# Moving SBUF tiles to one start modulo 512 bytes

## The chip, the core and the metric

The kernel runs on one core of one Trainium2 chip. The metric is device time in microseconds (us), from runs of the whole kernel. TensorE (PE) multiplies matrices and loads their stationary operands ("weight loads", PEld), VectorE is DVE, ScalarE is ACT, GpSimd is POOL, and SP issues most DMA transfers. SBUF is the on-chip memory: 128 partitions, in each of which every tile has the same start address and the same number of bytes. A "position" below is a tile's start address modulo 512 bytes.

## The reference

One layer of a decoder trunk on 1024 tokens of width 1024, all in float32. Two branches read the normed input, gates merge them, and a second gated input is added:

```python
h = rms_norm(x, g_pre[i])
proj = h @ w_in[i]
s5_x, s5_g, lru_x, lru_g, gate_s, gate_l = jnp.split(proj, IN_SPLITS, axis=-1)
y_s = s5_ssm(s5_x, ...)                       # 32 groups of 16 channels, 64 complex states each
glu_a, glu_b = jnp.split(jax.nn.gelu(y_s) @ w_glu[i], 2, axis=-1)
y_s = glu_a * jax.nn.sigmoid(glu_b) * jax.nn.silu(s5_g)
z_s = y_s @ w_bs[i]
c = causal_depthwise_conv(lru_x, conv_w[i], conv_b[i])
y_l = rg_lru(c, ...)                          # 10 heads of 128 channels, two 128x128 gates each
z_l = (y_l * jax.nn.silu(lru_g)) @ w_bl[i]
merged = jax.nn.sigmoid(gate_s) * z_s + jax.nn.sigmoid(gate_l) * z_l
x = x + rms_norm(merged @ w_out[i], g_post[i])
x = x + (p[i] @ w_ple[i]) * jax.nn.sigmoid(x @ w_ple_gate[i])
```

## The kernel before

**Matmuls.** Channels lie on the partitions and tokens along the free axis, in two halves of 512. Every large operand is split into a high and a low part (float32r), and each product is made of three matmuls by the helper `three` (lines 314 to 318): high weight by high operand (L316), then high by low and low by high (both L318). Such a matmul has a stationary block `wq` of 128x128 and a moving operand of 128x512. TensorE runs them one after another, in the order in which the code is written; while one streams, the weights of the next are loaded.

**Stages**, in the trace's order: `ps_ple` (the second input's product) to 25 us; the norm; `ps_u` and `ps_L` (input projection, S5 part and light gates) from 38 to 325 us, with the S5 scan between them; `ps_rx`/`ps_rg` (the LRU branch, head by head) to 565 us, with two gate products `pg` in each head that read the tile `chl`; the back projections `bX`, `bZ`, `bW`, `bV`, with the GLU `ps_eb`/`ps_ea` between them, to 711 us; `ps_F` to 755 us; the output projection `oX` to `oW`, with seven-product schemes that read sums of quarters (`bT`, `mT`, `bB`, `mB`); and the last gate `ps_pg`, which reads `x1hl`, one half of the tokens after the other.

**S5.** For each of 8 groups of heads, `s5_main` gives TensorE three short sets of plain float32 matmuls between those of `ps_L`: `pkt` (L925, reads `ca` and `bb`), `pin` (L936, reads `U` and the page `wn`) and `py` (L980 and L981, reads `U`, `toep`, `q` and `ca`).

**Where tiles lie.** Pools take SBUF from two ends. From the low end come the reserved DMA area (16384 bytes), four small constants, the pool `const` (`ones`, `ident`, `halfpi`, `cp_t` and two more), the raw weights `wraw`, the split weights `wq` (a ring of 6 tiles of 4096 bytes) and 14 pages of 8192 bytes. After `tc.swap_default_side()` pools take space from the high end downward, from address 229344: first the S5 pools `sk`, `ev` and `wk`, later, once these are closed, `l1` (the LRU's tiles, `chl` among them), then the pages 14 to 18. A tile takes its own bytes, rounded up to 32. So a tile that is not a multiple of 512 bytes shifts the position of all tiles behind it. These are the starts modulo 512 of what TensorE reads, from the allocation of the built program:

| operand | read by | before | after the change |
|---|---|---|---|
| `wq` (all weight blocks of `three`) | every 128x512 matmul | 160 | 480 |
| pages 0 to 13: `hB`, `ys`, `mB`, `yl`, geo0 and geo1, most of `bT`, `bB`, `x1hl` | `ps_L`, `ps_rx`, `ps_rg`, `ps_F` and others | 160 | 480 |
| `chl` | `pg` | 480 | 480 |
| pages 14 to 18: geo2 and geo3, T2 of `bT`, B22 of `bB`, T2 and T4 of `mT` | half of `ps_eb` and `ps_ea`; one product in each scheme | 480 | 480 |
| low part of `x1hl` for the second gate half (pages 14, 15) | `ps_pg` from 881 us | 480 | 480 |
| `U`, `q` | `pin`, `py` | 256 | 480 |
| `wn` (pages 2, 3) | `pin` | 160 | 480 |
| `toep` | `py` | 480 | 480 |
| `ca` (slices 576 bytes apart, some 64 further on) | `pkt`, `py` | tiles at 256 and 0 | tiles at 480 |
| `bb` (slices 64 bytes apart) | `pkt` | 288 | 480 |
| `ones`, `ident` | warm-up, norm sums | 128 | 448 |

The low and high parts of `wq`, and the 512-element quarters of a page, are whole multiples of 512 bytes apart and share their tile's position.

Of the kernel before, what the change touches and what calls it, by code (L numbers as in the profile page):

```python
# [9 lines left out]
F32 = mybir.dt.float32  # L10
# [7 lines left out]
P = 128  # L18
NT = 1024
HT = 512  # L20
# [115 lines left out]
class Weights:  # L136
# [99 lines left out]
    def next(self):  # L236
        self.make(self.pos)
        self.lows(self.pos)
        t = self.done[self.pos]
        n = QUADS[self.pos][3]  # L240
        self.pos += 1
        return [(t[:, 0, b, :], t[:, 1, b, :]) for b in range(n)]
# [10 lines left out]
def tile_hybrid_trunk(  # L253
# [34 lines left out]
    def cst(shape, name, value=None, dt=F32):  # L288
        t = const.tile(shape, dt, name=name)
        if value is not None:  # L290
            V.memset(t, value)
        return t

    ones = cst([P, P], "ones", 1.0)
    ident = cst([P, P], "ident")
    make_identity(nc, ident)
# [26 lines left out]
    def bank(name):  # L323
        return pp.tile([P, HT], F32, tag="pp", name=name)
# [131 lines left out]
    sk = s5x.enter_context(tc.tile_pool(name="sk", bufs=1))  # L456
# [22 lines left out]
    ET = mybir.EngineType  # L479
    ctx.enter_context(tc.manual_schedule(engines={ET.PE, ET.DVE, ET.Activation, ET.Pool}))  # L480

    sgn = sk.tile([P, 1], F32, name="sgn")
    bb = sk.tile([P, 512], F32, name="bb")
    d_skip = sk.tile([16, 32], F32, name="d_skip")
    r8 = sk.tile([P, 16], F32, name="r8")
    sinp = sk.tile([P, 160], F32, name="sinp")
# [340 lines left out]
    wk = s5x.enter_context(tc.tile_pool(name="wk", bufs=1))  # L827
# [46 lines left out]
    def s5_load(hb):  # L874
        if hb > 7:
            return
        t = page(2 + hb % 2, f"wn{hb}", F32).rearrange("p (s r n) -> p s r n", s=2, r=2)
        for r in range(2):
            nc.sync.dma_start(t[:, 0, r],
                              pt_d[r, :, HT * hb:HT * hb + HT].unsqueeze(0).to_broadcast([16, 8, HT]))  # L880
        nc.sync.dma_start(
            t[:, 1].rearrange("p r n -> p (r n)"),
            sbt[:, NT * hb:NT * hb + NT].unsqueeze(1).to_broadcast([16, 8, NT]))
        U = wk.tile([P, 4, P], F32, tag="U", name=f"U{hb}", bufs=2)
        nc.sync.dma_start(U, u_d[hb // 2][4 * (hb % 2):4 * (hb % 2) + 4].rearrange("g c j k -> (c j) g k"))
        wload[hb] = t, U

    def powers(t, hb, sl):
        return t[:, sl, 4 * hb:4 * hb + 4].rearrange("p d g -> p g d").unsqueeze(3)

    def s5_out_weights(hb):
        if hb == 0:
            G.tensor_tensor(cc[:, 0], cc[:, 0], sgn.to_broadcast([P, 512]), ALU.mult)
        ca = wk.tile([P, 4, 9, 16], F32, tag="ca", name=f"ca{hb}", bufs=2)
        s5["ca", hb] = ca
        t9 = wk.tile([P, 576], F32, tag="kt", name=f"t9_{hb}").rearrange("p (g d c) -> p g d c", g=4, d=9)
        pr, pi = (powers(t, hb, slice(0, 9)).to_broadcast([P, 4, 9, 16]) for t in (pw_r, pw_i))
        c1, c2 = (t[:, 4 * hb:4 * hb + 4, :].unsqueeze(2).to_broadcast([P, 4, 9, 16]) for t in (c_1, c_2))
        G.tensor_tensor(ca, pr, c1, ALU.mult)
        G.tensor_tensor(t9, pi, c2, ALU.mult)  # L900
        G.tensor_tensor(ca, ca, t9, ALU.subtract)

    def s5_main(hb, table, before):
        b, i0, g0 = hb // 2, 2 * hb, 4 * (hb % 2)
        ta = wk.tile([P, 2, 2, P], F32, tag="ta", name=f"ta{hb}")
        tb = wk.tile([P, 2, 2, P], F32, tag="tb", name=f"tb{hb}")
        tt = s5["tt", hb]
        ca = s5["ca", hb]
        wn, U = wload.pop(hb)
        V.tensor_tensor(wn[:, 0], wn[:, 0], wn[:, 1], ALU.mult)  # L910
        win = wn[:, 0, 0].rearrange("p (g n) -> p g n", g=4)
        V.tensor_tensor(wn[:, 0, 0], wn[:, 0, 0], wn[:, 0, 1], ALU.subtract)
        dd = wk.tile([16, 4, 16], F32, tag="dd", name=f"dd{hb}")
        G.tensor_tensor(
            dd, ident[:16, :16].unsqueeze(1).to_broadcast([16, 4, 16]),
            d_skip[:, 4 * hb:4 * hb + 4].unsqueeze(2).to_broadcast([16, 4, 16]), ALU.mult)
        yield
        before()
        s5_load(hb + 1)
        yield  # L920

        kt = wk.tile([P, 576], F32, tag="kt", name=f"kt{hb}")[:16, :HT].rearrange("p (g m) -> p g m", g=4)
        ps = px.tile([P, HT], F32, tag="px", name=f"pkt{hb}")
        for g in range(4):
            T.matmul(ps[32 * g:32 * g + 16, :P], bb_1[:, 4 * hb + g, :],  # L925
                     ca[:, g, 0:8, :].rearrange("p d c -> p (d c)"), start=True, stop=True, tile_position=(0, 32 * g))
        for g in range(4):
            S.activation(kt[:, g, :], ps[32 * g:32 * g + 16, :P], AF.Copy)
        V.tensor_tensor(kt[:, :, 0:16], kt[:, :, 0:16], dd, ALU.add)
        for j in range(8):  # L930
            nc.sync.dma_start(toep[j::8, :, 16 * j:P], kt[:, :, 0:P - 16 * j])
        yield

        pin = px.tile([P, 2, 2, P], F32, tag="px", name=f"pin{hb}")
        for g in range(4):
            T.matmul(pin[:, g // 2, g % 2, :], win[:, g, :], U[:, g, :], start=True, stop=True)  # L936
        next(table, None)
        yield

        pq = wk.tile([P, 4, P], F32, tag="pq", name=f"pq{hb}").rearrange("p (r i) n -> p r i n", r=2)  # L940
        for g2 in range(2):
            for r in range(2):
                S.activation(pq[64 * g2:64 * g2 + 64, r], pin[64 * r:64 * r + 64, :, g2, :], AF.Copy)
        q = wk.tile([P, 2, 2, P], F32, tag="q", name=f"q{hb}")
        cosb = tt[:, 0].unsqueeze(1).to_broadcast([P, 2, 2, P])
        sinb = tt[:, 1].unsqueeze(1).to_broadcast([P, 2, 2, P])
        V.tensor_tensor(ta, pq, cosb, ALU.mult)
        V.tensor_tensor(tb, pq, sinb, ALU.mult)
        V.tensor_tensor(q[:, 0], ta[:, 0], tb[:, 1], ALU.add)
        V.tensor_tensor(q[:, 1], ta[:, 1], tb[:, 0], ALU.subtract)  # L950
        if hb < 7:
            s5_out_weights(hb + 1)
        yield

        for r in range(2):
            for i in range(2):
                V.tensor_tensor_scan(q[:, r, i], r8[:, i0 + i:i0 + i + 1].to_broadcast([P, P]), q[:, r, i], 0.0,
                                     ALU.mult, ALU.add)
        next(table, None)
        e = P - 1  # L960
        V.tensor_tensor(ta, q, cosb, ALU.mult)
        V.tensor_tensor(tb, q, sinb, ALU.mult)
        yield

        V.memset(q[:, :, :, 0:1], 0.0)
        for g2 in range(2):
            s = slice(64 * g2, 64 * g2 + 64)
            V.tensor_tensor(q[:64, :, g2, 1:], ta[s, 0, :, :e], tb[s, 1, :, :e], ALU.subtract)
            V.tensor_tensor(q[64:, :, g2, 1:], ta[s, 1, :, :e], tb[s, 0, :, :e], ALU.add)
        next(table, None)  # L970
        yield

        def finish():
            for _ in table:
                pass
            ysb = wk.tile([P, 4, P], F32, tag="ysb", name=f"ysb{hb}")
            ps = px.tile([P, HT], F32, tag="px", name=f"py{hb}")
            for g in range(4):
                o_ = ps[:, g * P:(g + 1) * P]
                T.matmul(o_, toep[:, g, :], U[:, g, :], start=True, stop=False)  # L980
                T.matmul(o_, ca[:, g, 1:9, :].rearrange("p d c -> p (d c)"), q[:, g // 2, g % 2, :],  # L981
                         start=False, stop=True)
            S.activation(ysb.rearrange("p g k -> p (g k)"), ps, AF.Gelu_apprx_tanh)
            for g in range(4):
                nc.sync.dma_start(y_d[b][:, g0 + g], ysb[:, g])

        return finish
# [319 lines left out]
    for p_ in range(4):  # L1307
        m, u = 2 * p_, bu[:, p_, :]
# [163 lines left out]
    def mixt(row, h):  # L1472
        if mix[h][row // 4] is None:
            mix[h][row // 4] = quarter(page(PG[((0, 2), (18, 11))[h][row // 4]], f"mix{h}{row // 4}", F32))
        return mix[h][row // 4][:, row % 4, :]
# [141 lines left out]
    for name, row in (("T4", 1), ("T4", 3), ("T4", 5), ("T4", 7), ("B21", 4), ("B21", 6)):  # L1617
        c, ps = mixt(row, 0), bank(f"oV{row}")
# [76 lines left out]
```

## Time and profile before

| what | value |
|---|---|
| median of 3 runs | 932.56 us (932.4 to 933.21) |
| profiled execution, first to last instruction (span) | 930.6 us |
| the median less that span (around it: start and end of the execution) | 1.96 us |
| granted TensorE clock, mean | 0.999 of full speed |
| TensorE busy | 923.1 us, 4228 matmuls |
| DVE, ACT, POOL busy | 625.0, 469.6, 150.3 us |
| DMA moved | 134.21 MB, mean 144 GB/s |

The profile lists one execution. For the profiled execution nothing but its span is listed; its full time is taken as the span and the 1.96 us around it. A matmul's own duration there (389 ns and more) is longer than its share of TensorE's time, since each begins while the one before is still draining. What a matmul costs in a row of them is the distance from its start to the start of the next, and that is read from the start times in the timeline.

### The profile page before, as it was taken

The page shows a single profiled execution, that of the slowest core. Times are in us where ns is not written, and L with a number is a line of the kernel's source. Part 1 is how long each engine was busy: PE and PEld are TensorE (multiplying, and loading weights), DVE is VectorE, ACT ScalarE, POOL GpSimd, SP SyncE. Part 2 cuts the span into 40 slices and gives each one's busy share as a digit, 9 for nine tenths or more (in the row PEclk, how much of TensorE's full clock was granted, in tenths as well). Part 3 has the DMA queues.
Part 4 walks back from the last instruction along what each step waited for, and adds up shares of the span by engine and source line. Part 5 has one row for each costly group of instructions (what it writes and reads, how often), then busy time and mean ns, then how long its engine had stood idle before and what let it go on. Part 6 is the DMA issues. An engine that isn't in the chain of part 4 may idle for free.

```text
span 930.6 us, 11716 instructions
## 1 busy us (share of the span) xinstructions
PE 923.1 (99%) x4228; PEld 759.7 (82%) x4228; DVE 625.0 (67%) x977; ACT 469.6 (50%) x714; POOL 150.3 (16%) x159
## 2 busy tenths in 40 slices
PE   9999999999999999999999999999999999999997
PEld 7888888888888888888888888888888887887876
DVE  6985566666664446776666667687862798886863
ACT  6643233444443257666666668444434355558531
POOL 1318012212220000000000000022322126422100
PEclk9999999999999999999999999999999999999999
DMA  9745456554623211111111117811479965499951
GB/s 356 277 126 158 126 141 168 173 166 138 178 90 107 74 29 52 51 51 45 52 51 51 52 44 208 296 41 57 141 261 238 271 164 203 122 244 231 301 181 52
DMA packets 70442, 134.21 MB, mean 144 GB/s; under 512 B 18416, under 2 KB 32880, under 8 KB 70384
## 3 DMA queue, kind: packets, MB, share of 16 engines
q1 hardware_dynamic: 64768, 122.72, 41.5%
q0 software_dynamic: 5472, 10.49, 6.5%
q8 instruction: 33, 0.54, 0.2%
q10 hardware_dynamic: 144, 0.26, 0.1%
q14 instruction: 25, 0.20, 0.1%
HBM read 95.30 MB, written 27.53 MB: 132 GB/s over the span
## 4 chain that ended last, share of the span: by engine, by line
PE 96%; DVE 2%; issue 0%; DMA 0%; ACT 0%
PE ps_L L318 16%; PE ps_L L316 8%; PE ps_rg L318 8%; PE ps_rx L318 8%; PE ps_pg L318 6%; PE ps_rx L316 4%; PE ps_rg L316 4%; PE ps_F L318 3%; PE ps_u L318 3%; PE bZ L318 3%; PE ps_pg L316 3%; PE pg L318 2%; PE bW L318 2%; PE bX L318 2%; PE ps_ple L318 2%; PE ps_ea L318 2%
## 5 line engine op out<-in xcount | busy, mean ns | idle before, releaser
L318 PE MATMUL ps_L<-hB,wq 128*128 128x512 f32 x640 | 197.4, 390 | 0.0
L318 PEld LDWEIGHTS ps_L<-hB,wq 128*128 128x128 f32 x640 | 120.2, 188 | 24.5
L316 PE MATMUL ps_L<-hB,wq 128*128 128x512 f32 x320 | 127.0, 397 | 0.0
L222 ACT ACTIVATE wq<-wraw 128x512 fp32r<-128x512 f32 (+1 forms) x188 | 112.5, 614 | 24.3 <-issue 9.4
L234 DVE TENSOR_TENSOR wq<-wraw,wq 128x512 fp32r<-128x512 f32 (+1 forms) x152 | 104.0, 700 | 3.2 <-ACT wq L222 3.2
L318 PE MATMUL ps_rg<-hB,wq 128*128 128x512 f32 x320 | 98.7, 390 | 0.0
L318 PE MATMUL ps_rx<-hB,wq 128*128 128x512 f32 x320 | 98.7, 390 | 0.0
L318 PE MATMUL ps_pg<-x1hl,wq 128*128 128x512 f32 x240 | 75.2, 394 | 0.5 <-DVE x1hl L1371 0.5
L316 PEld LDWEIGHTS ps_L<-hB,wq 128*128 128x128 f32 x320 | 60.1, 188 | 13.4 <-issue 1.7
L318 PEld LDWEIGHTS ps_rg<-hB,wq 128*128 128x128 f32 x320 | 60.1, 188 | 12.9
L318 PEld LDWEIGHTS ps_rx<-hB,wq 128*128 128x128 f32 x320 | 60.1, 188 | 12.9
L1075 DVE SCALAR_TENSOR_TENSOR c<-ps_rx,cp_t,c 128x1023 f32<-128x1023 f32 (+2 forms) x30 | 38.5, 1282 | 47.6 <-ACT c L1073 46.9
L194 POOL TENSOR_TENSOR wS<-wraw 128x512 f32<-128x512 f32 x8 | 11.9, 1486 | 356.8 <-DMA wraw<-w_blocks 349.4
L316 PE MATMUL ps_rx<-hB,wq 128*128 128x512 f32 x160 | 62.5, 391 | 0.0
L316 PE MATMUL ps_rg<-hB,wq 128*128 128x512 f32 x160 | 62.5, 391 | 0.0
L318 PEld LDWEIGHTS ps_pg<-x1hl,wq 128*128 128x128 f32 x240 | 44.7, 188 | 11.8 <-DVE x1hl L1371 1.8
L1012 ACT ACTIVATE sg<-ps_L 128x1024 f32<-128x1024 f32 x20 | 20.5, 1026 | 59.6 <-issue 52.5
L226 POOL DMA_DIRECT2D wq<-wraw x36 | 31.8, 883 | 100.7 <-ACT wq L225 68.7
L316 PE MATMUL ps_pg<-x1hl,wq 128*128 128x512 f32 x120 | 47.1, 393 | 0.0
L318 PE MATMUL ps_u<-hB,wq 128*128 128x512 f32 x128 | 39.7, 392 | 0.4 <-DVE hB L733 0.4
L318 PE MATMUL ps_F<-ys,wq 128*128 128x512 f32 x128 | 39.4, 389 | 0.0
L1083 ACT ACT_TABLE_LOAD x9 | 11.5, 1283 | 51.2 <-DVE yr L1112 51.2
(360 smaller groups left out, 1930.4 us busy)
## 6 DMA issues: line engine op xcount, KB each, us to landing
wraw<-w_blocks SPq DMA_DIRECT2D x95, 512.0 KB
wq<-wraw POOLq DMA_DIRECT2D x36, 256.0 KB, 5.5
xt<-x_t SPq DMA_DIRECT2D x8, 512.0 KB
ple_d<-ple_sb SPq DMA_DIRECT2D x8, 512.0 KB
wn<-sbt SPq DMA_DIRECT2D x8, 512.0 KB
sgl_d<-sg SPq DMA_DIRECT2D x8, 512.0 KB
wn<-pt_d SPq DMA_DIRECT2D x16, 256.0 KB
sgs_d<-sg SPq DMA_DIRECT2D x8, 512.0 KB
```

What stands on the lines that cost most here:

```text
L194: G.tensor_tensor(s[name], s[a], s[b], op)
L222: nc.scalar.activation(hi, src, AF.Copy)
L226: nc.gpsimd.dma_start(lo.bitcast(F32), src, accum_op=ALU.add)
L234: self.nc.vector.tensor_tensor(lo, src, hi.bitcast(F32), ALU.subtract)
L316: T.matmul(ps, wh, xh, start=start, stop=False, skip_group_check=more)
L318: T.matmul(ps, a, b, start=False, stop=stop and a is (wh if xl_last else wl), skip_group_check=more)
L1012: S.activation(t, ps, AF.Sigmoid)
L1075: V.scalar_tensor_tensor(c[:, d:], ps[:, :NT - d], w_[3 - d], c[:, d:], ALU.mult, ALU.add)
L1083: S.activation(sq, ps, AF.Sigmoid)
```

## The change

A tile `phase` of 80 floats (320 bytes), which nothing uses, is taken from the pool `const` ahead of `ones`, so all that lies behind it on the low side is 320 bytes higher. In the S5 pools the tiles `sgn`, `bb`, `ca`, `kt`/`t9` and `dd` are taken larger and used in part, so that they take whole multiples of 512 bytes (`sgn` and `bb` bring the small tiles of `sk` to such a multiple together).

```diff
+    cst([P, 80], "phase")
     ones = cst([P, P], "ones", 1.0)
...
-    sgn = sk.tile([P, 1], F32, name="sgn")
-    bb = sk.tile([P, 512], F32, name="bb")
+    sgn = sk.tile([P, P], F32, name="sgn")[:, :1]
+    bb = sk.tile([P, 592], F32, name="bb")[:, :512]
...
-        ca = wk.tile([P, 4, 9, 16], F32, tag="ca", name=f"ca{hb}", bufs=2)
+        ca = wk.tile([P, 640], F32, tag="ca", name=f"ca{hb}", bufs=2)[:, :576].rearrange("p (g d c) -> p g d c", g=4, d=9)
...
-        t9 = wk.tile([P, 576], F32, tag="kt", name=f"t9_{hb}").rearrange("p (g d c) -> p g d c", g=4, d=9)
+        t9 = wk.tile([P, 640], F32, tag="kt", name=f"t9_{hb}")[:, :576].rearrange("p (g d c) -> p g d c", g=4, d=9)
...
-        dd = wk.tile([16, 4, 16], F32, tag="dd", name=f"dd{hb}")
+        dd = wk.tile([P, P], F32, tag="dd", name=f"dd{hb}")[:16, :64].rearrange("p (g c) -> p g c", g=4)
...
-        kt = wk.tile([P, 576], F32, tag="kt", name=f"kt{hb}")[:16, :HT].rearrange("p (g m) -> p g m", g=4)
+        kt = wk.tile([P, 640], F32, tag="kt", name=f"kt{hb}")[:16, :HT].rearrange("p (g m) -> p g m", g=4)
```

No instruction is added, removed or moved: on all five queues the same instructions stand in the same order with the same shapes. Only addresses differ.

## The prediction

> **What bounds the kernel.** I read the page first: busy time of the engines, granted clock, and the chain that ended last.
>
> ```profile
> PE 923.1 (99%) x4228; PEld 759.7 (82%) x4228; DVE 625.0 (67%) x977; ACT 469.6 (50%) x714; POOL 150.3 (16%) x159
> PEclk9999999999999999999999999999999999999999
> PE 96%; DVE 2%; issue 0%; DMA 0%; ACT 0%
> ```
>
> TensorE is busy for 99% of the span, at the full clock throughout, and 96% of the chain is TensorE. Next, the view of who waited for whom, for TensorE alone:
>
> ```profile
> PE warm L497 <- DVE halfpi L291: 1.1, 1, 1.1
> PE ps_ple L316 <- ACT wq L222: 0.6, 1, 0.6
> PE ps_pg L318 <- DVE x1hl L1371: 0.5, 1, 0.5
> PE ps_u L318 <- DVE hB L733: 0.4, 1, 0.4
> PE oY L318 <- DVE wq L234: 0.3, 1, 0.3
> ```
>
> 2.9 us of idle time in all. So the time is the number of matmuls times the distance between their starts, and the change can only matter through that distance. It removes and adds no matmul; the question is whether the start of an operand modulo 512 bytes sets the pace. The timeline answers it. First the longest stretch with one position: `ps_F`, whose moving operand `ys` and weights `wq` both start at 160. The groups of that stretch give the count, the timeline the ends:
>
> ```profile
> L318 PE MATMUL ps_F<-ys,wq 128*128 128x512 f32 x128 | 39.4, 389 | 0.0
> L316 PE MATMUL ps_F<-ys,wq 128*128 128x512 f32 x64 | 24.9, 389 | 0.0
> ...
> 711.67 0.39 PE L316 MATMUL ps_F<-ys,wq 128*128 128x512 f32 x1
> ...
> 755.19 0.39 PE L316 MATMUL oX<-mB,wq 128*128 128x512 f32 x1
> ```
>
> 192 matmuls in 755.19 - 711.67 = 43.52 us: 226.67 ns each. I call this the settled pace. Next a place in the LRU branch where six matmuls read `chl` (480) between long runs on `hB` (160), the weights being at 160 all the time. Only the first matmul of each three is shown, so a row is three matmuls behind the one above:
>
> ```profile
> 400.41 0.39 PE L316 MATMUL ps_rx<-hB,wq 128*128 128x512 f32 x1
> ...
> 401.09 0.39 PE L316 MATMUL ps_rx<-hB,wq 128*128 128x512 f32 x1
> ...
> 401.77 0.40 PE L316 MATMUL pg<-chl,wq 128*128 128x512 f32 x1
> ...
> 402.47 0.39 PE L316 MATMUL pg<-chl,wq 128*128 128x512 f32 x1
> ...
> 403.16 0.40 PE L316 MATMUL ps_rx<-hB,wq 128*128 128x512 f32 x1
> ...
> 403.85 0.40 PE L316 MATMUL ps_rx<-hB,wq 128*128 128x512 f32 x1
> ...
> 404.55 0.40 PE L316 MATMUL ps_rx<-hB,wq 128*128 128x512 f32 x1
> ...
> 405.24 0.39 PE L316 MATMUL ps_rx<-hB,wq 128*128 128x512 f32 x1
> ...
> 405.93 0.39 PE L316 MATMUL ps_rx<-hB,wq 128*128 128x512 f32 x1
> ...
> 406.61 0.39 PE L316 MATMUL ps_rx<-hB,wq 128*128 128x512 f32 x1
> ```
>
> The steps are 0.68, 0.68, then 0.70 and 0.69 for `chl`, and then, back on `hB`, 0.69, 0.70, 0.69, 0.69, and 0.68 again. Two readings follow. Matmuls of one shape at one clock run slower while weights and moving operand differ in position. And the slowness outlives the difference by some ten matmuls whose operands are again both at 160. So it is no fixed price of an address: two streams, the moving operand of one matmul and the weights of the next, fall into step with each other when their positions agree, are thrown out of step when they don't, and need about ten matmuls to settle.
>
> **The change part by part.** *The low side 320 bytes higher.* `wq` and pages 0 to 13 go from 160 to 480, where `chl` and pages 14 to 18 already are. If what counts is the difference between the two streams, every 128x512 matmul then runs at 226.67 ns. What that takes away, by places:
>
> LRU: from 401.77 to 406.61 are 21 matmuls in 4.84 us; settled they take 21 x 0.22667 = 4.76. One visit to `chl` costs 0.08 us, two in each of ten heads: 20 x 0.08 = 1.60 us.
>
> GLU, T2 and the last gate, where operands on the pages 14 to 18 take turns with the low pages:
>
> ```profile
> 598.73 0.40 PE L316 MATMUL ps_eb<-geo,wq 128*128 128x512 f32 x1
> ...
> 637.46 0.40 PE L316 MATMUL ps_ea<-geo,wq 128*128 128x512 f32 x1
> ...
> 640.22 0.39 PE L316 MATMUL bZ<-bT,wq 128*128 128x512 f32 x1
> ...
> 642.97 0.40 PE L316 MATMUL bW<-bT,wq 128*128 128x512 f32 x1
> ...
> 645.74 0.39 PE L316 MATMUL bV<-yl,wq 128*128 128x512 f32 x1
> ```
>
> ```profile
> 900.64 0.39 PE L316 MATMUL ps_pg<-x1hl,wq 128*128 128x512 f32 x1
> ...
> 903.42 0.40 PE L316 MATMUL ps_pg<-x1hl,wq 128*128 128x512 f32 x1
> ```
>
> From 598.73 to 637.46 stand seven periods of 24 matmuls, twelve on geo2 and geo3 and twelve on geo0 and geo1: 38.73 us for 168 against 38.08 settled, 0.65 us, or 0.09 for a period. From there to 645.74 are 24 at position 480 and twelve at 160: 8.28 against 8.16, 0.12 us. Each of the later products of twelve on pages 14 to 18 in the back projection (B22 four times, T2 three times more), followed by at least 18 at 160, is priced as a GLU period: 7 x 0.09 = 0.63. In the output projection T2 comes four times the same way, 0.36. T4 comes six times with norm work between, so it gets the settled part alone: a second product in a row at 480 takes from 640.22 to 642.97, twelve in 2.75 us or 229.2 ns, 0.03 us over, together 0.18. In the last gate's second half one matmul of each three reads the low part of `x1hl` at 480: from 900.64 to 903.42 are four threes in 2.78 us against 2.72, 0.015 each. Seven output rows of eight are 56 threes: 0.84 us. Its last row (256-wide matmuls) has no matched row to compare and stands at 0, in any case under 0.3 us for 48 of them if they too differ by some 5 ns.
>
> Sum: 1.60 + 0.65 + 0.12 + 0.63 + 0.36 + 0.18 + 0.84 = 4.38 us.
>
> *The padded S5 tiles.* `U`, `q`, `wn`, `toep` then share 480; the slices of `ca` and `bb` still lie 64 or 576 bytes apart and do not. The three S5 sets in each of 8 groups throw `ps_L` out of step:
>
> ```profile
> 206.07 0.62 PE L318 MATMUL ps_L<-hB,wq 128*128 128x512 f32 x2
> ...
> 207.91 0.39 PE L316 MATMUL ps_L<-hB,wq 128*128 128x512 f32 x1
> ...
> 209.36 0.63 PE L318 MATMUL ps_L<-hB,wq 128*128 128x512 f32 x2
> ...
> 211.20 0.39 PE L316 MATMUL ps_L<-hB,wq 128*128 128x512 f32 x1
> ...
> 213.00 0.62 PE L318 MATMUL ps_L<-hB,wq 128*128 128x512 f32 x2
> ...
> 214.15 0.39 PE L316 MATMUL ps_L<-hB,wq 128*128 128x512 f32 x1
> ```
>
> After `py` and after `pkt` eight matmuls take 1.84 us instead of 1.81, after `pin` five take 1.15 instead of 1.13: 0.08 us for a group, 0.6 us in all. It could go entirely (-0.6), or the short recovery after `pin` could become as long as that after the others (0.01 x 8, +0.1; I keep +0.3). The nearest row is a stall that has nothing to do with positions, inside the first gate half, where all operands are at 160:
>
> ```profile
> 841.95 0.73 PE L318 MATMUL ps_pg<-x1hl,wq 128*128 128x512 f32 x2 [0.47 <-DVE x1hl L1371]
> 842.53 0.39 PE L316 MATMUL ps_pg<-x1hl,wq 128*128 128x512 f32 x1
> ...
> 843.31 0.39 PE L316 MATMUL ps_pg<-x1hl,wq 128*128 128x512 f32 x1
> ...
> 843.99 0.39 PE L316 MATMUL ps_pg<-x1hl,wq 128*128 128x512 f32 x1
> ```
>
> There too the first three matmuls after the stall take 0.78 us instead of 0.68. An interruption alone costs steps, whatever the addresses, so I take 0 for the S5 tiles, with ends -0.6 and +0.3.
>
> *Other engines and DMA* get the same instructions on moved addresses; old and new starts are both 32 beyond a multiple of 64 bytes. They are off the chain (DVE 67%, ACT 50%), so a per cent on one of them is hidden under TensorE, except in the DVE steps that TensorE waits for (0.4, 0.5 and 0.3 us above). Those start from TensorE's own products and move with it. I keep 0.3 us of the gain as what may be lost there.
>
> The sum against the profiled execution: 930.6 - 4.4 = 926.2 us of span. With the 1.96 us around it, which the change doesn't touch, 928.2 us; the same as 932.56 - 4.38.
>
> **The rivals.** *No effect of addresses: 932.6 us.* Two streams that never meet would not care where they start, and the uneven steps would be an effect of `pg`'s other neighbours, ACT or DVE reading at the same time. Against it: the step changes exactly at the first matmul of the other position in the LRU and in the GLU alike, and `ps_F` holds 226.67 ns over 192 matmuls. The Trainium skill speaks for this rival: the page "TensorE: Matmul & The Clock Gate", Part 2, step 1, has TensorE read SBUF through two independent ports, so that loading the next weights takes nothing from the running matmul, and "SBUF — State Buffer", Who interferes with whom, says "PE and ACT never wait on anyone." By that rule the change gives 932.6; the trace's 226.67 against 229.2 ns for one shape at one clock disagrees with it.
>
> *Position 480 itself is slow: about 938 us, the other side.* No row has weights at 480, so the settled pace of 480 with 480 is not shown. If the moving operand's own place sets the 229.2 ns of the settled bT row, all 128x512 matmuls get it. Of the 4228, 48 of the last row, 64 of `pin`, 64 of `pkt`, 128 of `py` and 84 of warm-up, norm and transposes are smaller; of the 3840 left, some 464 read 480 today. 3376 x 2.5 ns = 8.4 us more, less the some 1.9 us of recoveries back at 160 and 1.0 of entries and alternation: 5.5 us more. It decides from 4.38 us / 3840 = 1.1 ns a matmul, that is, as soon as 480 with 480 settles above 227.8 ns. For it: that nothing shows this pair. Against it: back at 160 with 160 the pace stays slow for ten matmuls, so it hangs on the streams' step and not on an address.
>
> *Part of it only: about 930.5 us.* The change does not make all positions equal: `ca`, `bb` and the norm's `ones` stay off, and a longer period than 512 bytes may count besides. Half the 4.38 us would stay. Against it: in the trace, `yl`, `bT` and `ys` at 160 follow each other on different pages with no loss.
>
> **How the numbers follow.** Full effect 0.70, part of it 0.08, none 0.08, slow at 480 0.14. A difference under 0.2% (1.9 us) can't be told from none. Full effect with its ends (-0.6 and +0.3 of S5, 0.3 lost to DVE, 0.3 of the 256-wide row, and runs that spread by some 0.4) is 927.2 to 929.6, faster by 0.3 to 0.6%. Part of it lies on the edge of 0.2%, 0.05 beyond and 0.03 within. So faster 0.75, the same 0.11, slower 0.14. The range goes from 926.9 up to the no-effect case at 932.6 and leaves out the slow case.
>
> **What the profile after would show.** Right: `pg`, `ps_ea` and the later `ps_pg` with mean matmul durations of 389 ns as `ps_F` has, threes at 0.68 us through the LRU, and the LRU's heads shorter by 0.16 us each. Slow at 480: `ps_F`'s 192 matmuls over 43.9 us. No effect: the steps 0.70 and 0.69 around `pg` again. S5: if the padding counts, 1.81 us for the eight matmuls behind `py`. The prediction fails if the settled pace is a matter of absolute place, or if two equal positions at 480 fall into another step than at 160.

## The result and the profile after

The changed kernel takes 928.47 us (928.02 to 929.08, 5 runs) against 932.53 us (932.26 to 933.21, 5 runs), 4.06 us less: ratio 0.9956, 95% interval 0.9944 to 0.9968. The profiled execution's span went from 930.6 to 926.4 us, 4.2 us less. The change adds a line to the code above the helper, so L316 and L318 are now L317 and L319.

From the page of the kernel after, busy time and chain; then who waited for whom, for TensorE:

```profile
PE 918.5 (99%) x4228; PEld 759.9 (82%) x4228; DVE 624.9 (67%) x977; ACT 469.1 (51%) x714; POOL 150.1 (16%) x159
...
PE 91%; DVE 4%; issue 2%; DMA 1%; POOL 1%; ACT 1%; POOLq 0%; DVEq 0%; ACTq 0%
```

```profile
PE warm L498 <- DVE halfpi L291: 1.1, 1, 1.1
PE ps_ple L317 <- DVE p_hi L524: 0.7, 1, 0.7
PE ps_pg L319 <- DVE x1hl L1372: 0.5, 1, 0.5
PE ps_u L319 <- DVE hB L734: 0.4, 1, 0.4
PE oY L319 <- DVE wq L234: 0.3, 1, 0.3
PE ps_pg L319 <- DMA wq<-wraw: 0.2, 1, 0.2
```

TensorE is busy for 4.6 us less with the same 4228 matmuls, and every other engine is as busy as before. The chain has a smaller share of TensorE because ahead of short waits in the output projection and the last gate it was followed along the engines that these waits are for; the idle time of TensorE is 3.2 us, about as before (2.9). So the time did not come from a wait. The steps between the starts of two 128x512 matmuls say where it came from. Those of up to 245 ns, which hold no stall, lose 5.11 us against the settled pace in the trace before and 0.79 in the trace after, 4.32 us less; the longer ones, with a stall, hold 8.46 us beyond it in both.

The timeline at the same place in the LRU, the first matmul of each three:

```profile
399.60 0.39 PE L317 MATMUL ps_rx<-hB,wq 128*128 128x512 f32 x1
...
400.28 0.39 PE L317 MATMUL ps_rx<-hB,wq 128*128 128x512 f32 x1
...
400.96 0.39 PE L317 MATMUL pg<-chl,wq 128*128 128x512 f32 x1
...
401.64 0.39 PE L317 MATMUL pg<-chl,wq 128*128 128x512 f32 x1
...
402.32 0.39 PE L317 MATMUL ps_rx<-hB,wq 128*128 128x512 f32 x1
...
403.00 0.39 PE L317 MATMUL ps_rx<-hB,wq 128*128 128x512 f32 x1
...
403.68 0.39 PE L317 MATMUL ps_rx<-hB,wq 128*128 128x512 f32 x1
```

All steps are 0.68 us. TensorE goes to `chl` and back with no loss. The groups of the GLU and of `pg` say the same in one number, the mean duration (the last one ahead of the second bar), which was 391 to 396 ns and is now the 389 of `ps_F`. Before:

```profile
L318 PE MATMUL pg<-chl,wq 128*128 128x512 f32 x80 | 24.9, 393 | 0.0
...
L316 PE MATMUL pg<-chl,wq 128*128 128x512 f32 x40 | 15.8, 396 | 0.0
```

After:

```profile
L319 PE MATMUL pg<-chl,wq 128*128 128x512 f32 x80 | 24.6, 389 | 0.0
L319 PE MATMUL ps_eb<-geo,wq 128*128 128x512 f32 x64 | 19.7, 389 | 0.0
...
L317 PE MATMUL pg<-chl,wq 128*128 128x512 f32 x40 | 15.6, 389 | 0.0
```

By stages, from the start of the first matmul of one to that of the next (us, from the two timelines). The starts that bound the LRU and the GLU with the back projection, before (that of `ps_F`, 711.67, stands in the prediction) and after:

```profile
300.65 0.39 PE L316 MATMUL ps_rx<-hB,wq 128*128 128x512 f32 x1
...
568.81 0.39 PE L316 MATMUL bX<-bB,wq 128*128 128x512 f32 x1
...
596.01 0.39 PE L316 MATMUL ps_eb<-geo,wq 128*128 128x512 f32 x1
```

```profile
300.32 0.39 PE L317 MATMUL ps_rx<-hB,wq 128*128 128x512 f32 x1
...
566.88 0.39 PE L317 MATMUL bX<-bB,wq 128*128 128x512 f32 x1
...
594.08 0.39 PE L317 MATMUL ps_eb<-geo,wq 128*128 128x512 f32 x1
...
708.32 0.39 PE L317 MATMUL ps_F<-ys,wq 128*128 128x512 f32 x1
```

| from, to | before | after | less | forecast |
|---|---|---|---|---|
| start, `ps_L` | 77.99 | 77.81 | 0.18 | 0 |
| `ps_L`, `ps_rx` (with S5) | 222.66 | 222.51 | 0.15 | 0 (-0.3 to 0.6) |
| `ps_rx`, `bX` (LRU) | 268.16 | 266.56 | 1.60 | 1.60 |
| `bX`, `ps_eb` | 27.20 | 27.20 | 0 | 0 |
| `ps_eb`, `ps_F` (GLU, back projection) | 115.66 | 114.24 | 1.42 | 1.40 |
| `ps_F`, `oX` | 43.52 | 43.52 | 0 | 0 |
| `oX`, `ps_pg` (output projection) | 79.10 | 78.73 | 0.37 | 0.54 |
| `ps_pg`, last row | 85.83 | 85.26 | 0.57 | 0.84 |
| last row, to its last matmul's start | 5.54 | 5.63 | -0.09 | 0 |

The first row of the table can't be read as an effect of the change: in the profiles of `e_phase`, `e_s5pad`, `e_at160` and `e_d256` below, that stage takes 77.52 to 78.39 us, so a difference of 0.18 lies within what it varies by.

### The profile page after: what moved, and what is told of

It is laid out like the page before. It is cut to its first block, busy times and chain, and to the rows that moved or that the text cites. A ratio compares the mean times of both kernels' runs of the same rounds, so it can differ in the third digit from the quotient of the medians.

```text
span 926.4 us, 11716 instructions
## 1 busy us (share of the span) xinstructions
PE 918.5 (99%) x4228; PEld 759.9 (82%) x4228; DVE 624.9 (67%) x977; ACT 469.1 (51%) x714; POOL 150.1 (16%) x159
## 4 chain that ended last, share of the span: by engine, by line
PE 91%; DVE 4%; issue 2%; DMA 1%; POOL 1%; ACT 1%; POOLq 0%; DVEq 0%; ACTq 0%
PE ps_L L319 16%; PE ps_L L317 8%; PE ps_rg L319 8%; PE ps_rx L319 8%; PE ps_pg L319 4%; PE ps_rx L317 4%; PE ps_rg L317 4%; PE ps_u L319 3%; PE bZ L319 3%; PE ps_F L319 3%; PE pg L319 2%; PE ps_pg L317 2%; PE bW L319 2%; PE bX L319 2%; PE ps_ple L319 2%
## 5 line engine op out<-in xcount | busy, mean ns | idle before, releaser
L319 PE MATMUL ps_L<-hB,wq 128*128 128x512 f32 x640 | 197.4, 390 | 0.0
L319 PEld LDWEIGHTS ps_L<-hB,wq 128*128 128x128 f32 x640 | 120.2, 188 | 24.2
L317 PE MATMUL ps_L<-hB,wq 128*128 128x512 f32 x320 | 126.8, 396 | 0.0
L319 PE MATMUL ps_rx<-hB,wq 128*128 128x512 f32 x320 | 98.6, 389 | 0.0
L319 PE MATMUL ps_rg<-hB,wq 128*128 128x512 f32 x320 | 98.5, 389 | 0.0
L319 PE MATMUL ps_pg<-x1hl,wq 128*128 128x512 f32 x240 | 74.8, 391 | 0.8 <-DVE x1hl L1372 0.5
L317 PEld LDWEIGHTS ps_L<-hB,wq 128*128 128x128 f32 x320 | 60.1, 188 | 13.4 <-issue 1.7
L319 PEld LDWEIGHTS ps_rx<-hB,wq 128*128 128x128 f32 x320 | 60.1, 188 | 12.4
L319 PEld LDWEIGHTS ps_rg<-hB,wq 128*128 128x128 f32 x320 | 60.1, 188 | 12.4
L317 PE MATMUL ps_rx<-hB,wq 128*128 128x512 f32 x160 | 62.2, 389 | 0.0
L317 PE MATMUL ps_rg<-hB,wq 128*128 128x512 f32 x160 | 62.2, 389 | 0.0
L319 PEld LDWEIGHTS ps_pg<-x1hl,wq 128*128 128x128 f32 x240 | 44.9, 188 | 11.5 <-DVE x1hl L1372 1.2
L317 PE MATMUL ps_pg<-x1hl,wq 128*128 128x512 f32 x120 | 46.9, 391 | 0.0
L319 PE MATMUL ps_u<-hB,wq 128*128 128x512 f32 x128 | 39.8, 392 | 0.4 <-DVE hB L734 0.4
L319 PE MATMUL ps_F<-ys,wq 128*128 128x512 f32 x128 | 39.4, 389 | 0.0
```

Source lines behind the costliest of these rows:

```text
L317: T.matmul(ps, wh, xh, start=start, stop=False, skip_group_check=more)
L319: T.matmul(ps, a, b, start=False, stop=stop and a is (wh if xl_last else wl), skip_group_check=more)
```

## The experiments

Theory A is the prediction's: the weights of the next matmul and the moving operand of the running one are two streams that fall into step, and only the distance between their starts counts. Theory B: an operand's own place counts. Theory C: addresses have no effect.

### A map of distances

A kernel of its own, in which TensorE does nothing but stretches of 48 matmuls, each stretch with one moving start m and one distance d from the weights' start to it. `R` is float32r, `B` bfloat16; the diff is cut to the lines that matter:

```diff
+    for t, cols, ms in ((R, 512, (0, 160, 480)), (R, 256, (160,)), (B, 512, (0,))):
+        for m in ms:
+            for d in range(0, 512, 32):
+                yield t, cols, m, d
+    for m, d in ((160, 0), (480, 320)) * 3:
+        yield R, 512, m, d
...
+        o = (m - d) % 512
...
+            a, b = o // size + P * (k % 4), m // size + HT * (k % 2)
+            T.matmul(ps[:, :cols], wt[t][:, a:a + P], mv[t][:, b:b + cols], start=k == 0, stop=k == N_MM - 1)
```

> This kernel leaves the reference's work out altogether: it runs stretches of 48 matmuls (float32r 128x512, then 128x256, then bfloat16 128x512), each with one moving start m and one distance d from the weights' start to the moving start, modulo 512 bytes, and nothing else on TensorE. Theory A (two streams in step, only their distance counts): at d = 0 the settled pace is 226.7 ns for m = 0, 160 and 480 alike; d = 320 gives 229 ns once settled; the three curves over d are the same. Theory B (an operand's own place counts): the curves for m = 0, 160 and 480 differ, and 480 is slower than 160 by some 2.5 ns at equal d. Theory C (no effect of addresses; the uneven steps in the kernel come from other engines' reads): 226.7 ns in all stretches. What other distances give is not known; 224 ns is the shortest distance seen in the kernel, so some of them may lie below 226.7.

The timeline shows a row for each stretch; in its name stand m and d. The time from one row's start to the next, divided by 48, is the pace (with the settling at the stretch's begin):

```profile
186.36 11.08 PE L290 MATMUL m160d0x<-mv,wt 128*128 128x512 f32 x48
197.28 11.35 PE L290 MATMUL m160d32x<-mv,wt 128*128 128x512 f32 x48
208.47 11.16 PE L290 MATMUL m160d64x<-mv,wt 128*128 128x512 f32 x48
219.47 11.36 PE L290 MATMUL m160d96x<-mv,wt 128*128 128x512 f32 x48
230.67 11.36 PE L290 MATMUL m160d128x<-mv,wt 128*128 128x512 f32 x48
241.86 11.40 PE L290 MATMUL m160d160x<-mv,wt 128*128 128x512 f32 x48
253.10 11.36 PE L290 MATMUL m160d192x<-mv,wt 128*128 128x512 f32 x48
264.30 11.36 PE L290 MATMUL m160d224x<-mv,wt 128*128 128x512 f32 x48
275.50 11.05 PE L290 MATMUL m160d256x<-mv,wt 128*128 128x512 f32 x48
286.40 11.35 PE L290 MATMUL m160d288x<-mv,wt 128*128 128x512 f32 x48
...
364.62 11.09 PE L290 MATMUL m480d0x<-mv,wt 128*128 128x512 f32 x48
375.55 11.35 PE L290 MATMUL m480d32x<-mv,wt 128*128 128x512 f32 x48
...
633.37 10.53 PE L290 MATMUL m0d0x<-mb,wb 128*128 128x512 bf16 x47
643.74 10.52 PE L290 MATMUL m0d32x<-mb,wb 128*128 128x512 bf16 x47
654.10 10.52 PE L290 MATMUL m0d64x<-mb,wb 128*128 128x512 bf16 x47
```

The settled pace, from the last 24 steps of each float32r stretch (ns):

| d modulo 256 | 0 | 32 | 64 | 96 | 128 | 160 | 192 | 224 |
|---|---|---|---|---|---|---|---|---|
| 128x512, m = 0, 160 and 480 alike | 226.7 | 233.3 | 228.9 | 233.3 | 233.3 | 234.3 | 233.3 | 233.3 |
| 128x256, m = 160 | 120.0 | 116.7 | 117.8 | 120.0 | 118.6 | 117.3 | 113.3 | 118.3 |

Theory A holds and gains precision: the curve is the same for the three places of the moving operand, so B falls; no other engine worked beside it but for a copy of 0.7 us by DVE at the start of every eighth stretch, ahead of the steps counted here, and the transfers of input and output lie before and behind these steps, so C and other engines' reads fall. 480 with 480 settles at 226.7. 320 is 64 modulo 256, and gives the 228.9 that the kernel before showed on its high pages (229.2 by the rounded rows of the prediction, 228.9 by the exact starts). Two things are new: d counts modulo 256, not 512, and the bfloat16 stretches (one record of each 48 is missing in the trace) stand some 10.36 us apart at every distance, 215.8 ns a matmul; their weight blocks lie 256 bytes apart, so a distance there stands for itself modulo 256. A float32r matmul thus takes some 11 ns more than a bfloat16 one even at the best distance.

The map's last stretches repeat the kernel's own place: 160 with 160 behind a stretch that reads 480. By the exact starts in the trace, the last of them, from 842.98 us with no transfer and no other engine beside it, begins with steps of 234, 231, 233, 236, 224, 231, 236, 228, 233 and 231 ns and then keeps 226.7. Behind `chl`, from 403.16 us in the kernel before, stand the same ten. So the slow matmuls there are a matter of TensorE alone. Ten is not a fixed number: where distance 256 follows 224, it settles after one step.

### Each half of the change alone, and the same agreement at another place

The 320 bytes without the padded S5 tiles (against the kernel before; the diffs that follow are against the changed kernel):

```diff
+    cst([P, 80], "phase")
```

> The 320 bytes ahead of the low side alone, S5 tiles as before (U and q at 256, ca, kt and bb unpadded). Theory A: all but some 0.15 us of the gain, 928.6 us; settled 226.67 ns on hB, chl, geo; the eight matmuls behind py take 1.84 us as in the kernel before, not 1.82. Rival (the S5 tiles carry the gain, through the 24 places where S5 interrupts ps_L): about 932.

929.22 us, ratio 0.9963 (0.9949 to 0.9977), 0.6 us above what was expected; in its profile 0.6 us more stand ahead of `ps_L` than in the changed kernel's (78.39 against 77.81), in the stage that varies. Otherwise as theory A has it but for one point: behind `py` the settling took less, with `U` and `q` still at 256. The first row begins with the second matmul after `py`; the next two are five and eight matmuls behind it:

```profile
228.75 0.63 PE L319 MATMUL ps_L<-hB,wq 128*128 128x512 f32 x2
...
229.90 0.39 PE L317 MATMUL ps_L<-hB,wq 128*128 128x512 f32 x1
...
230.58 0.39 PE L317 MATMUL ps_L<-hB,wq 128*128 128x512 f32 x1
```

From 228.75 eight matmuls take 1.83 us, where 1.84 was expected. A row resolves no more than 0.01 us, but by the exact starts, summed over the 8 groups, these steps lose 0.08 us here, as in the full change, and 0.23 in the kernel before. So this gain comes from the low side too. The padding alone:

```diff
-    cst([P, 80], "phase")
```

> The padded S5 tiles alone, the low side as before (weights and pages 0 to 13 at 160, U, q, ca, toep, chl and pages 14 to 18 at 480). Theory A: 932.4 us, the steps 0.70 and 0.69 around pg unchanged, and behind py the settling takes as long as before or longer, since the weights behind it are at 160 and S5 at 480. Rival (the S5 tiles carry the gain): about 929.

932.81 us, ratio 1.0000 (0.9992 to 1.0009): no difference. Behind `py` the steps lose 0.23 us again, and around `pg` the loss stands as before (0.71, 0.68, then 0.70, 0.69):

```profile
401.63 0.40 PE L316 MATMUL pg<-chl,wq 128*128 128x512 f32 x1
...
402.34 0.39 PE L316 MATMUL pg<-chl,wq 128*128 128x512 f32 x1
...
403.02 0.40 PE L316 MATMUL ps_rx<-hB,wq 128*128 128x512 f32 x1
...
403.72 0.40 PE L316 MATMUL ps_rx<-hB,wq 128*128 128x512 f32 x1
...
404.41 0.40 PE L316 MATMUL ps_rx<-hB,wq 128*128 128x512 f32 x1
```

Agreement at 160 in place of 480, by 320 bytes that are the first taken at the high end:

```diff
-    cst([P, 80], "phase")
+    ctx.enter_context(tc.tile_pool(name="top", bufs=1)).tile([P, 80], F32, name="top")
```

> All positions agree as in the changed kernel, but at 160 instead of 480: 320 bytes are taken at the high end in place of the low end. Theory A (distance alone): 928.5 us, as the changed kernel, and 226.67 ns everywhere. Theory B (480 is a good or a bad place in itself): different from the changed kernel by 1 us or more.

928.94 us, ratio 0.9957 (0.9944 to 0.9969), within the interval of the changed kernel. The steps without a stall lose 0.91 us (0.79 in the changed kernel, 5.11 before). 480 is no place in itself.

### Modulo 256, and a distance that costs

64 bytes in place of 320 put weights and low pages at 224, the rest at 480:

```diff
-    cst([P, 80], "phase")
+    cst([P, 16], "phase")
```

> The changed kernel with 64 bytes at the low end in place of 320: weights and pages 0 to 13 at 224, chl, pages 14 to 18 and the S5 tiles at 480, so the distance from weights to moving operand takes the values 0 and 256. Theory A' (distance counts modulo 256, as the map of stretches has it: 226.7 ns at 0 and at 256): 928.5 us, every run of 128x512 matmuls at 226.67 ns. Rival (all operands must share one start modulo 512): the same unsettled steps around chl and pages 14 to 18 as before the change, 932 to 933 us.

928.85 us, ratio 0.9956 (0.9944 to 0.9969), and the steps around `chl` are 0.68 in a row (401.15 is the first on `chl`, 402.51 the first back on `hB`):

```profile
401.15 0.39 PE L317 MATMUL pg<-chl,wq 128*128 128x512 f32 x1
...
401.83 0.39 PE L317 MATMUL pg<-chl,wq 128*128 128x512 f32 x1
...
402.51 0.39 PE L317 MATMUL ps_rx<-hB,wq 128*128 128x512 f32 x1
...
403.19 0.39 PE L317 MATMUL ps_rx<-hB,wq 128*128 128x512 f32 x1
```

The operands need not share one start modulo 512; 256 does. Last, the weights alone 160 bytes away from everything else, with a tile `gap` allocated behind them:

```diff
+    ctx.enter_context(tc.tile_pool(name="gap", bufs=1)).tile([P, 40], F32, name="gap")
...
-    cst([P, 80], "phase")
+    cst([P, 40], "phase")
```

> The changed kernel with weights alone moved: 160 bytes ahead of them and 160 behind, so weights are at 320 and all moving operands at 480, distance 160 throughout. Theory A': each of the 3808 steps between 128x512 matmuls that the map has at 226.67 becomes 234.3 ns: 928.5 + 3808 x 7.6 ns = 957.5 us (ratio to before 1.027). Rival (only changes of position cost, a constant distance settles anywhere): 928 to 930. Rival (no effect of addresses): 932.5.

954.15 us, ratio 1.0226 (1.0210 to 1.0242): clearly slower, by the constant distance alone, which refutes both rivals. The pace was right: the 3757 steps that hold no stall lose 28.6 us against 226.67, 7.6 ns each. The total was 3.3 us too high. I had added the whole loss to a time that already held 0.8 us of settling, I had given it to the 51 steps with a stall too (0.4 us), and at the slower pace TensorE's stalls shrink: its steps over 245 ns hold 6.8 us beyond 226.67 ns, 8.5 in the changed kernel. Some 0.4 us stay unexplained, less than the runs of one kernel spread by. The waits in the output projection and the last gate are gone from the view:

```profile
PE warm L499 <- DVE halfpi L292: 1.1, 1, 1.1
PE ps_ple L318 <- ACT wq L222: 0.6, 1, 0.6
PE ps_u L320 <- DVE hB L735: 0.3, 1, 0.3
```

### Is there a faster pattern

A second map, of distances below 32 bytes, weights read with a step, distances that take turns, and narrower operands:

> Leaves the reference's work out: stretches of 48 float32r matmuls as in the first map, all with the moving operand at 256. Distances below 32 bytes (fine), weights taken with a step of 2 or 4 elements (pace, four), distances that take turns (turn, more, up, down, slow), and narrower moving operands (c448 and so on). Theory A' says that an unsettled pattern costs: turn, more, up, down and slow above 226.7 ns on average. Where weights are read with a step, theory A' has no number; if two readers of the same small pieces of memory get in each other's way, another step changes the pace, perhaps to less than 226.7; the nearest row, bfloat16 in the first map, is 215.8 at every distance. Narrower operands: columns / 2.4 plus 13.3 at the best distance if the loss is one per matmul.

Settled, nothing at 512 columns came below 226.7 ns. Distances of 4 to 28 bytes gave 228.3 (at 16) to 233.3; weights with a step of 2 elements 230.0 to 233.3, with a step of 4 235.0 to 240.0; distances in turn 230.0 to 233.3, above 226.7 as expected. The stepped weights also take starts 4 bytes apart in turn, so what the step alone costs is not shown. At distance 0, 480 columns took 216.7, 448 202.7 and 384 173.3 ns. From 256 to 512 columns (120.0 and 226.7) a column adds 0.417 ns, which leaves 13.3 ns for each matmul; 384 columns lie on that line, 448 and 480 some 3 ns above it. So most of the loss is one per matmul, and no narrower operand came out cheaper by the column. No faster version follows from this for the 128x512 matmuls. The last row's 48 matmuls of 128x256 would gain 6.7 ns each, 0.3 us, at d = 192; that is below what the runs tell apart, and it was not tried.

## Why the prediction was right

It gave 928.2 us; measured were 928.47.

*What bounds the kernel*: the number of matmuls times the time between their starts. Confirmed; `e_d160` keeps every matmul, changes only addresses, and moves the time by 26 us.

*The step of two streams and not a price of an address*: confirmed by the first map, in which three places give one curve. The evidence in the trace before, that the slowness outlived the difference by ten matmuls, was the right one to lean on, and the Trainium skill's rule ("TensorE: Matmul & The Clock Gate", Part 2, step 1) that loading weights takes nothing from the running matmul does not fit these float32r matmuls: 226.7 to 234.3 ns by the distance, with nothing else on TensorE. For bfloat16 the first map agrees with it, 215.8 ns at every distance.

*The low side*: 4.38 us forecast in the sum, and the LRU (1.60 and 1.60) and the GLU with the back projection (1.40 and 1.42) came out as worked out. The output projection gave 0.37 in place of 0.54. T2 saved 0.26 of 0.36: I had priced each visit with a full settling, though two of four contain a stall of their own. T4 saved 0.11 of 0.18: the prediction counts six of its products, but there are four (48 matmuls `oV<-mT`); the other two read B21, on low pages. The last gate gave 0.57 in place of 0.84, and there the pace did what was forecast: in the second half's full-width rows the steps without a stall lose 0.88 us before and 0.02 after. The stalls took the rest. In the second half they went from 0.35 us (a wait for `x1hl`) to nothing, while the first half's grew by 0.54, with a new one on a weight block (`PE ps_pg L319 <- DMA wq<-wraw` above), and its steps without a stall lose 0.09 more. The stalls move between the halves from profile to profile: the first half takes 46.97, 46.65 and 46.65 us in those of `e_at160`, `e_d256` and `e_phase`, with 0.15, 0.46 and 0.47 us of stalls in the second.

*The S5 tiles*, taken at 0: right for the padding (no measurable time), but 0.15 us came from the low side at this place, inside the range. The reason that the prediction gives is a row misread. The three matmuls behind the stall at 841.95 take 0.78 us because the second of them waits for `x1hl` again, which the view of the weight loads shows and that of the matmuls does not:

```profile
842.74 0.30 PEld L318 LDWEIGHTS ps_pg<-x1hl,wq 128*128 128x128 f32 x2 [0.26 <-DVE x1hl L1371]
```

That an interruption costs steps without any difference of positions is shown by the changed kernel instead: behind `pin`, which reads `U` and `wn` at 480 like all around it, the steps still lose 0.01 us a visit.

*The last row*, taken at 0: it lost 0.09, since 256-wide matmuls at distance 0 settle at 120.0 ns, in the map's worst place. Before, its low operands alternated between two distances and it ran at 117.8 ns. In `e_s5pad`, with the same positions, it settled at 120.0 and took 5.62 us: one pattern of distances can fall into more than one step.

*What is luck*: that the total came within 0.3 us. The 0.18 us ahead of `ps_L` and the 0.15 of S5, neither forecast, make up for a good part of what the output projection, the gate and the last row fell short by.

*Rivals*: slow at 480, refuted by the map and by `e_at160`; no effect, refuted by the result and by `e_d160`; part of it only, refuted by the stage table. That a period longer than 512 bytes might count was the wrong way round: it is 256.

What physically makes the step is not settled. The runs show that float32r matmuls have it and bfloat16 ones don't, that it goes by the distance, and that it has a period of 256 bytes; they do not show which reads meet. In the first map a weight load takes 188 ns for float32r and 98 for bfloat16; whether that matters was not tested.

## What to carry to other kernels

Where TensorE bounds a kernel, compare the distance between the starts of matmuls of one shape across the trace, not their busy time; an uneven step at full clock, with no wait, is a lead. Look at the waits of the weight loads too before calling a step free of waits. With float32r operands, give the stationary and the moving operand the same start modulo 256 bytes: one unfitting small tile ahead of a pool shifts everything behind it, and here 64 or 320 bytes of padding put it right. It is worth little unless the distance is a bad one throughout: 0.4% here, against 2.8% between `e_d160` and the changed kernel. Measure the map of one's own shape first, since 256 columns have their best distance elsewhere (192) than 512 columns (0).

## What the runs showed that I had not expected

The pace has a period of 256 bytes and its best distance is 0 for 512 columns (226.7 ns) but 192 for 256 columns (113.3, against 120.0 at 0). A constant distance can cost more than changing ones: 234.3 ns at 160, against 230 to 233 for patterns that take turns. And a slower TensorE gave back part of its loss elsewhere: 1.7 us less stalls at 954 us than at 928.
